# Modulation sums of a two-layer decoder trunk: scaling on ScalarE and accumulating DMAs instead of running sums on VectorE

## The chip, the cores and the metric

One core of one Trainium2 chip runs the whole kernel. The metric is the device time of one execution in microseconds (us); a time given for a kernel is the median of several runs. Five engines work beside each other, each with its own queue in order: TensorE (PE; the loads of its stationary operand are listed as PEld), VectorE (DVE), ScalarE (ACT), GpSimd (POOL) and SyncE (SP). SyncE issues nearly all DMAs of this kernel. Sixteen DMA engines carry them.

## The reference

The reference is a trunk of two layers on one sequence of 512 tokens with 2048 features, in float32. Layer 0 is differential attention with 8 heads and a SiLU gate; layer 1 is forgetting attention with 16 heads, on keys and values that are projected once from the stream. What the change touches is the modulation: a conditioning vector `c` gives, by matrix-vector products, a shift, a scale and a gate for each layer, and a shift and a scale for the shared keys and values.

```
c_act = silu(c)                                   # 1 x 2048
for l in range(2):
    mod = c_act @ w_mod[l] + b_mod[l]             # 2048 x 6144 for each layer
    shift, scale, gate = split(mod, 3)
    h = x * (1 + scale) + shift
    if l == 0:
        y = diff_attention(h, ...)
    else:
        mod = c_act @ w_mod_kv + b_mod_kv         # 2048 x 4096
        shift_kv, scale_kv = split(mod, 2)
        k, v, F = projections(x * (1 + scale_kv) + shift_kv)
        y = forgetting_attention(h, ..., k, v, F)
    x = layer_norm(alpha * x + gate * y)
```

## The kernel before

The contraction over 2048 features is cut into 16 k-tiles of 128. Large products are done in three matmuls each: an operand is split into a high part that TensorE takes as it is (`hi`, a cast on ScalarE) and the rest (`lo`, a subtraction on VectorE), and `products` adds high x high, low x high and high x low (lines 201 to 203).

Weights of the projections come through `WeightStream`: SyncE loads two k-tiles into a stage `wst` (four stages, line 59), ScalarE casts them into `whi` (line 106, three buffers), VectorE makes `wlo` (line 107, three buffers). `group` runs one projection block: eight such steps with four bursts of six matmuls each. After each burst, `tick` takes one prepared piece of attention work and a number `bg` of steps from the generator `background`. This is how the modulation is slipped in beside the matmuls.

The first 190 us make scale and shift of layer 0 with their own code. The rest of the modulation is made by two runs of the generator `mod_stream` (line 383), each over 12 column blocks of 512 columns:

- The first stream makes the gate of layer 0 and the shift and scale for keys and values, during layer 0's projections and attention (about 190 to 810 us). It loads two k-tiles at a time into `ms` (two buffers of 128 x 2 x 512).
- The second makes shift, scale and gate of layer 1, from the output projection of layer 0 on and through the projections of values (`vj`) and keys (`kj`), about 860 to 1325 us. It loads one k-tile at a time into `ms` (three buffers), and for loads 50 to 105 of the stream into buffers `msk` of a large pool, up to seven k-tiles ahead.

A block has one accumulator `macc` (128 x 512, two buffers). For each k-tile VectorE does one instruction: `macc = ms * cact[k] + macc` (line 420; the first k-tile of a block is a plain product, line 418), where `cact[k]` is a column of 128 scalars. A step of the generator is one k-tile. When 16 are done, `mod_rows` (line 440) transposes `macc` in 32 x 32 blocks into `mturn`, reduces along the rows into `mred`, and after four blocks one small matmul (line 460), an addition of the bias and a store to DRAM end one vector of 2048. The function `fold` later reads it back, in the second stream for the input of layer 1, and the gate is read back at the residual.

Outside the first stage the order of the instructions on each engine is chosen by a scheduler from the program's order and its dependencies; the sums are held in the program's order by `keep_in_program_order`. An engine executes its queue strictly in that order, so an instruction that waits holds up all that stand behind it. SyncE holds up the weight loads in the same way.

Of the kernel before, what the change touches and what calls it, by code (L numbers as in the profile page):

```python
# [137 lines left out]
def tile_yoco(  # L138
# [23 lines left out]
    nc = tc.nc  # L162
    V, S, PE, G = nc.vector, nc.scalar, nc.tensor, nc.gpsimd
# [19 lines left out]
    def acc_bank(name="acc"):  # L183
        return ps.tile([P, 512], F32, name=name, tag="acc", bufs=4)
# [4 lines left out]
    def tr_bank(name="tr"):  # L189
        return ps.tile([P, 512], F32, name=name, tag="tr", bufs=1)  # L190
# [39 lines left out]
    cact = const.tile([P, KT], F32, name="cact")  # L230
# [15 lines left out]
    rows = {}  # L246
# [44 lines left out]
    kk = Job(a_w_in, [(2048 + 128, 128), (2048 + 384, 128)])  # L291
# [88 lines left out]
        return const.tile([P, KT], F32, name=name)  # L380


    def mod_stream(segs, new_stage, new_acc, nk, deep=range(0), new_deep=None):

        todo = [(i, r) for i in range(len(segs)) for r in range(KT // nk)]
        loaded = {}
        summed = []

        def load(k):
            i, r = todo[k]
            src, col, _ = segs[i]
            t = new_deep() if k in deep else new_stage()
            rows = src[nk * r * P : nk * (r + 1) * P, col : col + 512]
            nc.sync.dma_start(t, rows.rearrange("(k p) n -> p k n", p=P) if nk > 1 else rows)
            loaded[k] = t

        def load_upto(k):
            n = len(loads)  # L400
            while n < len(todo) and n <= (k + 7 if n in deep else k + 2 // nk):
                load(n)
                loads.append(n)
                n += 1

        loads = []
        load_upto(-1)
        for k, (i, r) in enumerate(todo):
            load_upto(k)
            if r == 0:  # L410
                acc = new_acc()
            t = loaded.pop(k)
            for kk in range(nk):
                kt = nk * r + kk
                w = t[:, kk, :] if nk > 1 else t

                if kt == 0:
                    ins = V.tensor_scalar(acc, w, cact[:, 0:1], None, op0=ALU.mult)
                else:
                    ins = V.scalar_tensor_tensor(acc, w, cact[:, kt : kt + 1], acc, op0=ALU.mult, op1=ALU.add)  # L420
                tc.keep_in_program_order(ins)
                if kt == KT - 1:
                    summed.append(segs[i][2](acc))
                if kt in (1, 9) and summed:
                    if next(summed[0], None) is None:
                        summed.pop()
                yield
        for n, _ in enumerate(summed[0]):

            for _ in range(1 if n else 6):  # L430
                yield

    def four_ones(pool):

        t = pool.tile([P, P], F32, name="fours", tag="fours")
        for k in range(0, P, 32):
            S.copy(t[k : k + 32, 0:32], ident[k : k + 32, k : k + 32])
        return t[:, 0:32]

    def mod_rows(pool, fours, dst, bias, one):  # L440

        red = []

        def steps(n, acc):
            if n == 0:
                red.append(pool.tile([P, 64], F32, name="mred", tag="mred", bufs=2))
            t = pool.tile([P, 512], F32, name="mturn", tag="mturn", bufs=1)
            V.transpose(t, acc)  # L450
            V.tensor_reduce(
                red[0][:, 16 * n : 16 * n + 16], t.rearrange("p (j q) -> p j q", q=32), axis=mybir.AxisListType.X, op=ALU.add
            )
            if n == 3:
                row = pool.tile([64, 32], F32, name="mrow", tag="mrow", bufs=1)
                nc.sync.dma_start(row, bias.rearrange("(j q) -> j q", q=32))
            yield True
            if n == 3:
# [12 lines left out]
    with tc.tile_pool(name="start", bufs=2, reuse_waits="tile") as sp, tc.manual_schedule(engines=MANUAL):  # L471
# [10 lines left out]
        loads = []  # L482
# [319 lines left out]
    ap = actx.enter_context(tc.tile_pool(name="ap", bufs=1, reuse_waits="tile"))  # L802
    segs = []
    fours = four_ones(ap)
    for dst, src, col, bias, one in (
# [4 lines left out]
        steps = mod_rows(ap, fours, dst, bias[col : col + D], one)  # L810
        segs += [(src, col + 512 * f, partial(steps, f)) for f in range(4)]
    background = mod_stream(
        segs,
        lambda: ap.tile([P, 2, 512], F32, name="ms", tag="ms", bufs=2),
        lambda: ap.tile([P, 512], F32, name="macc", tag="macc", bufs=2),
        2,
    )
    dist = ap.tile([P, 512], F32, name="dist")
    G.iota(dist, pattern=[[-1, 512]], base=384, channel_multiplier=1, allow_small_or_imprecise_dtypes=True)
# [327 lines left out]
    def ktile(name):  # L1147
        return kpool.tile([P, T], F32, name=name, tag="K")
# [61 lines left out]
    def open_n():  # L1210
        nonlocal background
        actx.close()
        pool = nctx.enter_context(tc.tile_pool(name="npool", bufs=1, reuse_waits="tile"))
        zp.extend((pool, pool.tile([P, TB, D], F32, name="n"), pool.tile([P, TB, 4, 6], F32, name="nstats")))
        fours = four_ones(pool)
        segs = []
        for dst, col, one in ((mod_dram[1][0:1, :], 0, 0.0), (mod_dram[1][1:2, :], D, 1.0), (gate_dram[1], 2 * D, 0.0)):
            steps = mod_rows(pool, fours, dst, b_mod[1, col : col + D], one)
            segs += [(w_mod[1], col + 512 * f, partial(steps, f)) for f in range(4)]
        background = mod_stream(  # L1220
            segs,
            lambda: pool.tile([P, 512], F32, name="ms", tag="ms", bufs=3),
            lambda: pool.tile([P, 512], F32, name="macc", tag="macc", bufs=2),
            1,

            deep=range(50, 106),
            new_deep=lambda: ktile("msk"),
        )

    def end_of_sums():  # L1230
# [163 lines left out]
    acc = [acc_bank() for _ in range(TB)]  # L1394
# [4 lines left out]
    for i, (half, s) in enumerate(lag):  # L1399
# [299 lines left out]
```

## Time and profile before

| | us |
|---|---|
| median of three runs | 1944.55 |
| lowest and highest run | 1944.41, 1945.12 |
| span of the profiled execution | 1943.2 |
| TensorE busy | 1922.5 |
| VectorE busy | 1351.3 |
| ScalarE busy | 730.3 |
| GpSimd busy | 2.2 |

The span reaches from the first to the last instruction of one profiled execution. Consecutive matmuls overlap in the records (a matmul of 512 columns is recorded with some 0.39 us but they start every 0.23 us), so TensorE's busy time says that it always had one in hand, not how fast it worked. In a row of the groups, `out<-in` names the tile written and the tiles read, then come shapes, count, total busy time, the mean time of one in ns, and the time for which the engine stood idle just before, with whom it waited for. A row of DMA issues ends with the median time from issue to landing.

### The profile page before, as it was taken

Reading aid. Unit: us, or ns where it says so; the run is one execution under the profiler, and the core shown is the slowest. Engines: PE = TensorE matmul, PEld = TensorE weight load, DVE = VectorE, ACT = ScalarE, POOL = GpSimd, SP = SyncE. Lnnn points to the kernel's source line nnn. Section 1 sums busy time; section 2 is a strip of 40 time slices with the busy share of each in tenths; the row PEclk is TensorE's granted clock in tenths of the full one; section 3 lists DMA queues with packets and bytes.
Section 4 is the critical chain, followed back from the end, with each engine's and each line's share of the span. In section 5 each row is a group of like instructions: output and inputs, shape, how many; then the busy total and the mean of one; then the engine's idle time right before and its main releaser. Section 6 shows DMA issues by size and latency. Waiting matters only on the chain.

```text
span 1943.2 us, 25791 instructions
## 1 busy us (share of the span) xinstructions
PE 1922.5 (99%) x8973; PEld 1619.5 (83%) x8973; DVE 1351.3 (70%) x2514; ACT 730.3 (38%) x1250; POOL 2.2 (0%) x10
## 2 busy tenths in 40 slices
PE   8999999999999999999999999999999999999997
PEld 7888888888888888888889998888888888888886
DVE  6884588777676768567675657777566666677657
ACT  3546344323332334521273222224343434353123
POOL 0000000000000000000000000000000000000000
PEclk9999999999999999999999999999999999999999
DMA  9983466676767675377557756774355555554622
GB/s 339 383 300 115 151 187 201 210 230 188 239 192 225 202 237 167 121 241 225 171 174 256 266 187 214 251 260 158 118 154 148 153 155 154 152 171 153 222 91 105
DMA packets 351630, 382.19 MB, mean 197 GB/s; under 512 B 77926, under 2 KB 260860, under 8 KB 350732
## 3 DMA queue, kind: packets, MB, share of 16 engines
q1 hardware_dynamic: 348620, 376.35, 61.6%
q10 hardware_dynamic: 2880, 4.20, 0.6%
q8 instruction: 70, 1.15, 0.2%
q14 instruction: 60, 0.49, 0.1%
HBM read 348.65 MB, written 31.80 MB: 196 GB/s over the span
## 4 chain that ended last, share of the span: by engine, by line
PE 96%; DVE 3%; DMA 1%; issue 0%; ACT 0%; SPq 0%; DVEq 0%
PE acc L201 27%; PE acc L202 27%; PE acc L203 27%; PE acc L703 4%; PE sc L703 2%; PE o L201 1%; PE o L202 1%; PE o L203 1%; PE sc L203 1%; PE sc L202 1%; PE o L703 1%; PE sc L201 1%; DVE sacc L601 1%; PE tr L643 0%; PE tr L669 0%; PE tr L629 0%
## 5 line engine op out<-in xcount | busy, mean ns | idle before, releaser
L106 ACT CAST whi<-wst 128x1024 fp32r<-128x1024 f32 (+2 forms) x298 | 303.4, 1018 | 660.7 <-PE acc L203 353.2
L107 DVE TENSOR_TENSOR wlo<-wst,whi 128x1024 fp32r<-128x1024 f32 (+2 forms) x298 | 351.4, 1180 | 261.0 <-ACT whi L106 254.5
L201 PE MATMUL acc<-hh,whi 128*128 128x512 f32 x1184 | 463.5, 391 | 0.0
L202 PE MATMUL acc<-hl,whi 128*128 128x512 f32 x1184 | 461.8, 390 | 0.0
L203 PE MATMUL acc<-hh,wlo 128*128 128x512 f32 x1184 | 460.9, 390 | 0.0
L201 PE MATMUL acc<-whi,hh 128*128 128x512 f32 (+1 forms) x1168 | 444.4, 381 | 0.0
L202 PE MATMUL acc<-wlo,hh 128*128 128x512 f32 (+1 forms) x1168 | 442.3, 379 | 0.0
L203 PE MATMUL acc<-whi,hl 128*128 128x512 f32 (+1 forms) x1168 | 441.8, 378 | 0.0
L420 DVE SCALAR_TENSOR_TENSOR macc<-ms,cact,macc 128x512 f32<-128x512 f32 x307 | 229.1, 746 | 63.1 <-DMA ms<-in_w_mod_dram 41.1
L203 PEld LDWEIGHTS acc<-hh,wlo 128*128 128x128 f32 x1184 | 222.3, 188 | 47.6
L201 PEld LDWEIGHTS acc<-hh,whi 128*128 128x128 f32 x1184 | 222.5, 188 | 43.6 <-issue 0.6
L202 PEld LDWEIGHTS acc<-hl,whi 128*128 128x128 f32 x1184 | 222.4, 188 | 42.1
L203 PEld LDWEIGHTS acc<-whi,hl 128*128 128x128 f32 x1168 | 219.2, 188 | 36.5 <-DVE hl L1280 0.2
L201 PEld LDWEIGHTS acc<-whi,hh 128*128 128x128 f32 x1168 | 219.2, 188 | 34.8 <-DVE ztmp L1194 0.4
L202 PEld LDWEIGHTS acc<-wlo,hh 128*128 128x128 f32 x1168 | 219.3, 188 | 33.6 <-DVE wlo L107 0.3
L601 DVE SCALAR_TENSOR_TENSOR sacc<-sms,cact,sacc 128x512 f32<-128x512 f32 (+1 forms) x123 | 87.5, 712 | 5.9 <-DMA sms<-in_w_mod_dram 2.6
L880 ACT ACTIVATE e<-e,mn 128x128 f32<-128x128 f32 (+3 forms) x64 | 36.0, 563 | 113.5 <-DVE mn L876 99.6
L1504 ACT ACTIVATE eb<-eb,mnb 128x128 f32<-128x128 f32 (+1 forms) x64 | 36.0, 563 | 88.0 <-DVE mnb L1501 87.8
L876 DVE CUSTOM_DVE_ANT_0 e<-sc,bias 128x128 f32<-128x128 f32 (+3 forms) x64 | 31.0, 485 | 28.1 <-PE sc L203 27.8
L125 DVE TENSOR_TENSOR wlo<-wst,whi 128x768 fp32r<-128x768 f32 (+1 forms) x32 | 34.8, 1088 | 18.7 <-ACT whi L118 9.9
L703 PE MATMUL acc<-whi,hh 128*128 128x512 f32 x128 | 46.4, 394 | 0.0
L703 PE MATMUL acc<-whi,hl 128*128 128x512 f32 x128 | 45.9, 394 | 0.0
(285 smaller groups left out, 1999.0 us busy)
## 6 DMA issues: line engine op xcount, KB each, us to landing
wst<-in_a_w_in_dram SPq DMA_DIRECT2D x240, 256.0 KB, 4.1
ms<-in_w_mod_dram SPq DMA_DIRECT2D x136, 256.0 KB, 3.7
ms<-in_kv_w_mod_dram SPq DMA_DIRECT2D x64, 512.0 KB, 4.0
wst<-in_b_w_in_dram SPq DMA_DIRECT2D x128, 256.0 KB, 3.0
sms<-in_w_mod_dram SPq DMA_DIRECT2D x56, 512.0 KB, 7.7
wst<-in_kv_w_dram SPq DMA_DIRECT2D x40, 512.0 KB, 4.2
ms<-in_w_mod_dram SPq DMA_DIRECT2D x32, 512.0 KB, 4.5
wst<-in_a_w_out_dram SPq DMA_DIRECT2D x32, 512.0 KB, 4.4
```

The lines of the kernel that those rows point to most:

```text
L106: self.nc.scalar.copy(hi[:, :, :w], st[:, :, :w])
L107: self.nc.vector.tensor_tensor(lo[:, :, :w], st[:, :, :w], hi[:, :, :w].bitcast(F32), op=ALU.subtract)
L125: self.nc.vector.tensor_tensor(lo[:, :, :w], st[:, :, :w], hi[:, :, :w].bitcast(F32), op=ALU.subtract)
L201: PE.matmul(dst, lhs[0], rhs[0], start=start, stop=False)
L202: PE.matmul(dst, lhs[0], rhs[1], start=False, stop=False)
L203: PE.matmul(dst, lhs[1], rhs[0], start=False, stop=stop)
L420: ins = V.scalar_tensor_tensor(acc, w, cact[:, kt : kt + 1], acc, op0=ALU.mult, op1=ALU.add)
L601: V.scalar_tensor_tensor(acc, w, sc, acc, op0=ALU.mult, op1=ALU.add)
L703: PE.matmul(bank[n, bk], l, r, start=start, stop=stop, skip_group_check=True)
L876: V.tensor_tensor_reduce(out=e[:, :w], in0=sc[:, :w], in1=st["bias"][:, (3 - i) * P :], scale=-1.0, scalar=3.0e38, op0=ALU.add, op1=ALU.mi ...
L880: S.activation(e[:, :w], e[:, :w], AF.Exp, bias=mn, scale=-1.0, accum_out=rs)
L1504: S.activation(e[:, :w], e[:, :w], AF.Exp, bias=mn, scale=-1.0, accum_out=rs)
```

## The change

`mod_stream` now always loads two k-tiles at a time. The first pair of a block is loaded straight into the accumulator `macc`, which is now 128 x 2 x 512; the other seven pairs go into `ms`, 128 x 2 x 512 with two buffers, in both streams. ScalarE scales each half in place by its column of `cact`. When a pair other than the first is scaled, GpSimd issues one DMA from `ms` to `macc` that adds into its destination. The load of pair k+1 is issued when pair k is taken up; the separate, deeper buffers `msk` are gone. After a block, VectorE adds the two halves of `macc`, and one turn later transposes and reduces as before, in the accumulator's second half instead of `mturn`.

```diff
-    def mod_stream(segs, new_stage, new_acc, nk, deep=range(0), new_deep=None):
+    def mod_stream(segs, new_stage, new_acc):
-        todo = [(i, r) for i in range(len(segs)) for r in range(KT // nk)]
+        todo = [(i, r) for i in range(len(segs)) for r in range(KT // 2)]
...
         def load_upto(k):
-            n = len(loads)
-            while n < len(todo) and n <= (k + 7 if n in deep else k + 2 // nk):
-                load(n)
-                loads.append(n)
-                n += 1
+            for n in range(len(loads), min(k + 1, len(todo))):
+                i, r = todo[n]
+                src, col, _ = segs[i]
+                t = loaded[n] = new_stage() if r else new_acc()
+                rows = src[2 * r * P : 2 * (r + 1) * P, col : col + 512]
+                nc.sync.dma_start(t, rows.rearrange("(k p) n -> p k n", p=P))
+                loads.append(n)
...
+        load_upto(1)
         for k, (i, r) in enumerate(todo):
-            load_upto(k)
+            load_upto(k + 1)
+            t = loaded.pop(k)
             if r == 0:
-                acc = new_acc()
-            t = loaded.pop(k)
-            for kk in range(nk):
-                kt = nk * r + kk
-                w = t[:, kk, :] if nk > 1 else t
-                if kt == 0:
-                    ins = V.tensor_scalar(acc, w, cact[:, 0:1], None, op0=ALU.mult)
-                else:
-                    ins = V.scalar_tensor_tensor(acc, w, cact[:, kt : kt + 1], acc, op0=ALU.mult, op1=ALU.add)
-                tc.keep_in_program_order(ins)
-                if kt == KT - 1:
-                    summed.append(segs[i][2](acc))
-                if kt in (1, 9) and summed:
+                acc = t
+            for kk in range(2):
+                kt = 2 * r + kk
+                tc.keep_in_program_order(S.activation(t[:, kk, :], t[:, kk, :], AF.Copy, scale=cact[:, kt : kt + 1]))
+                if kk and r:
+                    G.dma_start(acc, t, accum_op=ALU.add)
+                if kt in (3, 5, 11) and summed:
                     if next(summed[0], None) is None:
                         summed.pop()
                 yield
+            if r == KT // 2 - 1:
+                summed.append(segs[i][2](acc))
...
-            t = pool.tile([P, 512], F32, name="mturn", tag="mturn", bufs=1)
-            V.transpose(t, acc)
+            t = acc[:, 1, :]
+            V.tensor_tensor(acc[:, 0, :], acc[:, 0, :], acc[:, 1, :], op=ALU.add)
+            yield True
+            V.transpose(t, acc[:, 0, :])
...
-            lambda: pool.tile([P, 512], F32, name="ms", tag="ms", bufs=3),
-            lambda: pool.tile([P, 512], F32, name="macc", tag="macc", bufs=2),
-            1,
-            deep=range(50, 106),
-            new_deep=lambda: ktile("msk"),
+            lambda: pool.tile([P, 2, 512], F32, name="ms", tag="ms", bufs=2),
+            lambda: pool.tile([P, 2, 512], F32, name="macc", tag="macc", bufs=2),
```

How the change stands in the queues is best seen where the second stream meets the projection of the keys. First ScalarE's queue there. Before, in the first key blocks, it holds the weight casts (line 106) and the copies of finished banks (line 1340). The names in brackets are the counters waited for: DMAHW those of SyncE's DMAs, DMASW those of GpSimd's, the others the engines'.

```order
L1340 COPY kT<-acc 128x512 [waits PE_49]
L106 COPY whi<-wst 128x1024 [waits DMAHW3_49,DVE_49,PE_49]
L106 COPY whi<-wst 128x1024 [waits DMAHW0_49,DVE_49,PE_49]
L106 COPY whi<-wst 128x1024 [waits DMAHW4_49,DVE_49,PE_49]
L106 COPY whi<-wst 128x1024 [waits DMAHW1_49,DVE_49,PE_49]
L106 COPY whi<-wst 128x1024 [waits DMAHW5_49,DVE_49,PE_49]
```

The same place after the change:

```order
L407 ACTIVATE ms<-ms,cact 128x512 [waits DMAHW3_49,DMASW3_49,Activation_49]
L407 ACTIVATE ms<-ms,cact 128x512
L106 COPY whi<-wst 128x1024 [waits DMAHW5_49,DVE_49,PE_49]
L407 ACTIVATE ms<-ms,cact 128x512 [waits DMAHW5_49,DMASW4_49,Activation_49]
L407 ACTIVATE ms<-ms,cact 128x512
L106 COPY whi<-wst 128x1024 [waits DMAHW7_49,DVE_49,PE_49]
L407 ACTIVATE ms<-ms,cact 128x512 [waits DMAHW0_49,DMASW5_49,Activation_49]
L407 ACTIVATE ms<-ms,cact 128x512
L106 COPY whi<-wst 128x1024 [waits DMAHW2_49,DVE_49,PE_49]
```

The two scalings of a pair (line 407) have moved in ahead of each weight cast, and the first of them waits for the load of its pair.

Next SyncE's queue in the same stage. Before, each weight load (line 59) stands among three or four loads of one k-tile (line 396), which wait for VectorE to have read the stage:

```order
L59 DMA wst<-in_kv_w_dram 128x2x512 [waits DVE_49]
L396 DMA ms<-in_w_mod_dram 128x512 [waits DMAHW4_49,DVE_49]
L396 DMA ms<-in_w_mod_dram 128x512 [waits DMAHW5_49,DVE_49]
L396 DMA ms<-in_w_mod_dram 128x512 [waits DMAHW6_49,DMAHW2_49,DVE_49]
L59 DMA wst<-in_kv_w_dram 128x2x512 [waits DVE_49]
```

After the change:

```order
L59 DMA wst<-in_kv_w_dram 128x2x512 [waits DVE_49]
L396 DMA ms<-in_w_mod_dram 128x2x512 [waits DMAHW4_49,DMASW6_49,Activation_49]
L59 DMA wst<-in_kv_w_dram 128x2x512 [waits DMAHW3_49,DVE_49]
L396 DMA ms<-in_w_mod_dram 128x2x512 [waits DMAHW0_49,DMASW7_49,Activation_49]
L59 DMA wst<-in_kv_w_dram 128x2x512 [waits DMAHW5_49,DVE_49]
L396 DMA ms<-in_w_mod_dram 128x2x512 [waits DMAHW6_49,DMAHW2_49,DMASW0_49]
L59 DMA wst<-in_kv_w_dram 128x2x512 [waits DMAHW7_49,DVE_49]
```

Between two weight loads there now stand one or two loads of a pair, and each waits for an accumulation (DMASW) that GpSimd issued.

GpSimd's queue was empty after its setup; in this stage it now holds:

```order
L409 DMA macc<-ms 128x1024 [waits DMASW0_49,DMAHW5_49,DVE_49,Activation_49]
L409 DMA macc<-ms 128x1024 [waits DMAHW7_49,DMASW0_49,Activation_49]
L409 DMA macc<-ms 128x1024 [waits DMAHW2_49,DMASW1_49,Activation_49]
L409 DMA macc<-ms 128x1024 [waits DMAHW4_49,DMASW2_49,Activation_49]
L409 DMA macc<-ms 128x1024 [waits DMAHW6_49,DMASW3_49,Activation_49]
```

Each waits for the one before it (DMASW counted up by one from row to row) and for ScalarE.

More of the change, by code (lines that the diff above doesn't have):

```diff
@@ L380, in cols @@
         return const.tile([P, KT], F32, name=name)
-    def mod_stream(segs, new_stage, new_acc, nk, deep=range(0), new_deep=None):
-        todo = [(i, r) for i in range(len(segs)) for r in range(KT // nk)]
[L388 to L397, printed above, removed]
-        def load_upto(k):
-            n = len(loads)
-            while n < len(todo) and n <= (k + 7 if n in deep else k + 2 // nk):
-                load(n)
+    def mod_stream(segs, new_stage, new_acc):
+        todo = [(i, r) for i in range(len(segs)) for r in range(KT // 2)]
+        loaded, loads, summed = {}, [], []
+        def load_upto(k):
+            for n in range(len(loads), min(k + 1, len(todo))):
[4 more added lines that the diff above has]
+                nc.sync.dma_start(t, rows.rearrange("(k p) n -> p k n", p=P))
@@ L403, in load_upto @@
                 loads.append(n)
-                n += 1
-        loads = []
-        load_upto(-1)
+        load_upto(1)
         for k, (i, r) in enumerate(todo):
-            load_upto(k)
+            load_upto(k + 1)
+            t = loaded.pop(k)
             if r == 0:
-                acc = new_acc()
-            t = loaded.pop(k)
-            for kk in range(nk):
-                kt = nk * r + kk
-                w = t[:, kk, :] if nk > 1 else t
-                if kt == 0:
-                    ins = V.tensor_scalar(acc, w, cact[:, 0:1], None, op0=ALU.mult)
-                else:
-                    ins = V.scalar_tensor_tensor(acc, w, cact[:, kt : kt + 1], acc, op0=ALU.mult, op1=ALU.add)
-                tc.keep_in_program_order(ins)
-                if kt == KT - 1:
-                    summed.append(segs[i][2](acc))
-                if kt in (1, 9) and summed:
+                acc = t
[5 more added lines that the diff above has]
+                if kt in (3, 5, 11) and summed:
@@ L814, in tile_yoco @@
         lambda: ap.tile([P, 2, 512], F32, name="ms", tag="ms", bufs=2),
-        lambda: ap.tile([P, 512], F32, name="macc", tag="macc", bufs=2),
-        2,
+        lambda: ap.tile([P, 2, 512], F32, name="macc", tag="macc", bufs=2),
     )
```

## The prediction

> **What bounds the kernel now.** I read the page's engine line first, then a table by stage, then TensorE's own waits in the stage where the two streams of sums run.
>
> ```profile
> span 1943.2 us, 25791 instructions
> PE 1922.5 (99%) x8973; PEld 1619.5 (83%) x8973; DVE 1351.3 (70%) x2514; ACT 730.3 (38%) x1250; POOL 2.2 (0%) x10
> ...
> 0.00:190.00 190.00, 182.47 (x847) 152.75 (x848) 136.85 (x199) 96.50 (x155) 2.17 (x10) 1.00 0.86 290
> 190.00:1330.00 1140.00, 1139.49 (x5379) 967.46 (x5378) 812.94 (x1549) 407.00 (x708) 0.00 (x0) 1.00 0.66 208
> 1330.00:1943.00 613.00, 600.57 (x2751) 499.31 (x2749) 401.53 (x767) 226.84 (x390) 0.00 (x0) 0.99 0.48 148
> ...
> PE sc L1286 <- ACT n L1261: 0.5, 1, 0.5
> ```
>
> The windows give start:end, length, busy time and count of PE, PEld, DVE, ACT and POOL, the granted clock, the DMA engines' busy share, GB/s. The sums lie in 190 to 1330 us. There TensorE is busy 1139.49 of 1140 us, and the last row is its only wait. So whatever VectorE is freed of, this stage can give back 0.5 us. The question is only whether the new route for the sums feeds ScalarE and SyncE as fast as TensorE consumes.
>
> **What is removed and added.** VectorE loses these groups:
>
> ```profile
> L420 DVE SCALAR_TENSOR_TENSOR macc<-ms,cact,macc 128x512 f32<-128x512 f32 x307 | 229.1, 746 | 63.1 <-DMA ms<-in_w_mod_dram 41.1 <-DMA ms<-in_kv_w_mod_dram 19.0
> L420 DVE SCALAR_TENSOR_TENSOR macc<-msk,cact,macc 128x512 f32<-128x512 f32 x53 | 39.7, 749 | 1.0
> L418 DVE TENSOR_SCALAR macc<-ms,cact 128x512 f32<-128x512 f32 x21 | 10.1, 479 | 1.2 <-DMA ms<-in_kv_w_mod_dram 1.2
> L1642 DVE TENSOR_TENSOR z<-nr,ztmp 128x512 f32<-128x512 f32 x16 | 10.5, 686 | 0.1
> L1062 ACT ACTIVATE ogs<-ogT,subg 128x512 f32<-128x512 f32 x14 | 9.1, 714 | 0.0
> ```
>
> 229.1 + 39.7 + 10.1 = 279 us (three more first products make 384 in all) go; 24 adds of one half to the other come, at 0.686 us (the L1642 row) 16 us. Both are worth nothing at the end: TensorE's matmuls cover them. Were they not covered, the 263 us would be the gain, but the 0.5 us row forbids that. ScalarE gains 384 scalings by a column; the nearest row is L1062, 0.714 us, so 274 us, and 407 + 274 = 681 of 1140 us is 60%. Its throughput is not the problem either.
>
> GpSimd's queue gains 168 accumulating DMAs of 512 KB (7 for each of 24 column blocks), and no row shows one. The loads become 192 of 512 KB instead of 288, but each of the 168 that fill a stage now waits for an accumulation. Call A the time from issuing an accumulation to its landing. Two waits repeat:
>
> *The chain*: accumulation r+1 reads and writes the tile that r writes, so it waits for r. One per A.
>
> *The ring*: there are two stage tiles. Load n needs the tile that accumulation n-2 reads; ScalarE needs load n; accumulation n needs ScalarE. Two accumulations per A + load + two scalings.
>
> ```profile
> ms<-in_kv_w_mod_dram SPq DMA_DIRECT2D x64, 512.0 KB, 4.0
> sms<-in_w_mod_dram SPq DMA_DIRECT2D x56, 512.0 KB, 7.7
> ms<-in_w_mod_dram SPq DMA_DIRECT2D x32, 512.0 KB, 4.5
> n_dram<-n SPq DMA_DIRECT2D x4, 1024.0 KB, 3.8
> out_dram<-z SPq DMA_DIRECT2D x7, 512.0 KB, 2.7
> ```
>
> (Last number: median us to landing.) A load is 4.2 (between 4.0 and 4.5), two scalings 1.4. The ring takes (A + 5.6)/2 for one accumulation, the chain A; the larger counts, T. They cross at A = 5.6.
>
> *The price of A*. From the two stores, another 512 KB costs 3.8 - 2.7 = 1.1 us, so 1.6 is fixed. An accumulation reads source and destination: 1.6 + 2 x 1.1 = 3.8 alone. It runs beside loads, and these take 4.0 to 4.5 where the store took 2.7: 1.3 to 1.8 us more for each 512 KB moved, 2.6 to 3.6 for two. That gives 6.4 to 7.4. I take **A = 6.6**, near the lower end because it starts in SBUF, as the cheaper stores do. Bounds: 2.7 (it costs no more than a store) and 1.6 + 2 x (7.7 - 1.6) = 13.8 (both halves move as slowly as the loads under full DMA). At 6.6 the chain decides, T = 6.6.
>
> The Trainium skill, "DMA: Bandwidth & Descriptors", section "Anatomy of one DMA — SWDGE (gpsimd) path", fits a transfer from GpSimd's queue at 2.0 us plus bytes over 436 GB/s. That is 3.2 us here for a plain copy; by it the ring would decide with T = 4.4 and the end would be 1961 us, an estimate from that page. No run so far shows it.
>
> **The pace it must keep.** One column block is 16 k-tiles and 7 accumulations, so a k-tile costs 7T/16 = 2.89 us at T = 6.6. The table shows how many k-tiles the kernel asks for now (DVE busy, its count, clock, DMA share, GB/s):
>
> ```profile
> 250.00:350.00 100.00, 21.63 (x30) 1.00 0.66 196
> 350.00:500.00 150.00, 45.23 (x62) 1.00 0.71 216
> 500.00:750.00 250.00, 70.98 (x98) 1.00 0.70 213
> 750.00:860.00 110.00, 9.39 (x13) 1.00 0.55 170
> 860.00:950.00 90.00, 28.35 (x39) 1.00 0.65 209
> 950.00:1025.00 75.00, 0.00 (x0) 1.00 0.51 165
> 1025.00:1050.00 25.00, 7.93 (x11) 1.00 0.77 257
> 1050.00:1150.00 100.00, 35.79 (x49) 1.00 0.77 259
> 1150.00:1200.00 50.00, 15.38 (x21) 1.00 0.58 178
> 1200.00:1325.00 125.00, 57.28 (x79) 1.00 0.75 249
> ...
> L106 ACT CAST whi<-wst 128x1024 fp32r<-128x1024 f32 x23 | 24.3, 1055 | 70.9 <-PE acc L202 66.3 <-DVE wlo L107 4.4
> ```
>
> k-tiles x 2.89 less the length: 62 make 179 us, 29 too many; 98: 283, 33; 39: 113, 23; 11: 32, 7; 49: 142, 42; 21: 61, 11; 79: 228, 103. The stretches with 30 and 13 k-tiles keep up. Sum 247 us. ScalarE and SyncE work in the order shown ahead of this text: behind a late scaling stand the whi casts that TensorE needs, behind a late load the weight loads. So lateness reaches TensorE one for one once ScalarE's lead is used up. That lead is two casts (three whi buffers; the last row, of 1200 to 1325 us, shows the casts waiting for TensorE to free one), at 125/23 = 5.4 us each 11 us, and it is filled again in the two slack stretches: three times 11 = 33 us off. 247 - 33 = **214 us**. The profiled execution spans 1943.2 and the median of the runs is 1.35 above it: 1943.2 + 214 + 1.35 = **2158 us**.
>
> By the bounds of A, in the same way: A = 2.7 gives T = 4.15, 1.82 us a k-tile; only the last stretch is late, by 18 - 11, so 1952. A = 13.8 is 6.04 us a k-tile: late by 1459 in all, so about 3370. Between them: A = 4.5 (T = 5.05) gives 1991; A = 8.9 is 624 - 33 = 591 us late, 2535.
>
> **The rivals.**
>
> *The accumulation is quick* (A under 4.5): 1952 to 1990. For it: the plain-copy fit of the Trainium skill's page named above, and the 2.7 us row. Against it: the stores of that row stand near the end, where the DMA engines are half idle. The ring still binds in the densest stretch.
>
> *It is slow* (A above 8.9): over 2535. For it: no row shows an adding DMA, nor one from GpSimd's queue. Against it: only the loads under full DMA, in the first stage, come near.
>
> *The 16 DMA engines are full* before chain or ring bind (A small, but all transfers late). Two moves of 1.1 us for each accumulation, on top of the shares in the table: 1200 to 1325 needs 0.75 x 125 + 34.6 x 2.2 = 170 us of all engines, 45 too many; 1050 to 1150 124, 24; the others 46 together (16, 19, 6, 5). 115 - 33 = 82: 2026 us. Deeper buffers would then not help. The Trainium skill, in the same page under "Issuing engines are not separate DMA queues", says that DMAs from all queues share the 16 engines, which speaks for it.
>
> *Not slower*: TensorE sees nothing. The place is the densest stretch: 79 k-tiles in 125 us ask for 1.58 us a k-tile, so T = 3.6 and, by the ring, A under 1.6 us, which is the fixed part of a store alone; the mechanism would be that loads and accumulations overlap more than the two tiles seem to allow. Then the time is 1944, at best 0.5 us less.
>
> **How the numbers follow.** The forecast (chain or ring, A from 4.5 to 8.9, 1990 to 2535, likeliest 2158) has 0.67; quick accumulation 0.06; slow 0.11; full DMA engines 0.10; not slower 0.06. The range 1985 to 2535 holds the forecast, the full engines and a little of the quick case, 0.8. A measurement here tells 0.2%, 4 us, from no change. Faster takes half of the not-slower case, 0.03, same the other half, 0.03; all else is slower, 0.94.
>
> **What would show it.** Right: POOL's DMAs from macc<-ms land in 4.5 to 8.9 us; SP's longest waits are loads of ms on them; ScalarE's idle time before ms<-ms,cact is on DMA and in the order of 200 us; TensorE loses its time between 350 and 750 us and, most of all, in the stretch that was 1200 to 1325, and nothing after the second stream. DMA share in those stretches stays under 1.0. Wrong: a DMA share at 1.0 with ring waits short (full engines); TensorE's waits naming VectorE (the adds or the transposes late); or a loss in the stage after 1330 us, where I expect none. If the landing of an accumulation is right but the time is not, the step from k-tiles to lateness is at fault.

## The result and the profile after

The change makes the kernel slower: 2366.94 us (median of 4 runs, 2363.09 to 2371.42) against 1944.48 us for the kernel before on the same chip (4 runs, 1943.96 to 1945.12). The ratio is 1.2173, with a 95% interval of 1.2159 to 1.2187. So 422 us were lost. The prediction was a loss of 214 us, 2158 us in all, in a range of 1985 to 2535: the range holds the time, and the loss came out nearly twice as large as forecast.

First the page of the kernel after: the span, the engines' busy time, the granted clock and the DMA engines' share in 40 slices, and the chain that ended last, by engine and by line.

```profile
span 2366.0 us, 25982 instructions
...
PE 2030.7 (86%) x8973; PEld 1682.8 (71%) x8973; DVE 1114.0 (47%) x2154; ACT 958.3 (41%) x1634; POOL 145.1 (6%) x178
...
PEclk9999998898988989998898888787779999999999
DMA  9964888888988978487758888787864445455632
...
PE 31%; DMA 29%; DVE 3%; issue 2%; ACT 2%; SPq 0%; POOLq 0%; DVEq 0%; ACTq 0%
DMA macc<-ms 24%; PE acc L201 9%; PE acc L202 9%; PE acc L203 9%; DMA ms<-in_w_mod_dram 3%; DMA e<-turned 1%; ACT ms L407 1%; ACT whi L106 1%; PE o L201 1%; DVE wlo L107 1%; PE o L202 1%; PE o L203 1%; PE sc L203 0%; PE sc L202 0%; PE sc L2
```

TensorE's busy time plus its idle time is the span. Before, 20.7 of 1943.2 us were idle; now 2366.0 - 2030.7 = 335.3 are. That is 314.6 us of the loss. The other 108 us (2030.7 - 1922.5) are busy time of the same 8973 matmuls, whose records became longer (391 ns on average before and 411 after in the largest group of line 201); they go with the slices where the clock row falls below 9. VectorE became freer by 237 us (1351.3 to 1114.0), and nothing came of it. The chain points to the cause: the DMAs from `ms` to `macc` alone hold 24% of the span, where the kernel before had no such thing. (The shares of the chain add up to some two thirds: it was not followed back to the start.)

The groups show what the added work does to its own engines: the scalings on ScalarE, GpSimd's DMA instructions, and VectorE's addition of the two halves (busy time, mean ns, idle time before them and its releaser).

```profile
L407 ACT ACTIVATE ms<-ms,cact 128x512 f32<-128x512 f32 x336 | 230.0, 716 | 628.0 <-DMA ms<-in_w_mod_dram 481.9
...
L409 POOL DMA_DIRECT2D macc<-ms x168 | 142.9, 851 | 1453.1 <-DMA macc<-ms 571.2
L438 DVE TENSOR_TENSOR macc<-macc 128x512 f32<-128x512 f32 x24 | 16.6, 692 | 163.3 <-DMA macc<-ms 163.3
```

The scaling costs 0.716 us, as the prediction took it from another row (0.714), and the addition of halves 0.692 (0.686). GpSimd's instruction, which no row had shown, takes 0.851 us of the engine, one for each DMA. The DMA issues and the queue give the price that everything hung on (packets, MB and share of the 16 engines for the queue; KB and median us to landing for the issues):

```profile
q0 software_dynamic: 24192, 88.09, 19.4%
...
macc<-ms POOLq DMA_DIRECT2D x168, 512.0 KB, 7.2
...
ms<-in_w_mod_dram SPq DMA_DIRECT2D x112, 512.0 KB, 4.1
...
ms<-in_kv_w_mod_dram SPq DMA_DIRECT2D x56, 512.0 KB, 3.9
```

An accumulation lands 7.2 us after its issue (4.4 at least, 9.8 at most). It keeps the 16 DMA engines busy for 19.4% x 2366.0 / 168 = 2.73 us. The waits show how this spreads (us in total, times, longest): GpSimd waits for its own last accumulation, ScalarE for the loads, VectorE's `wlo` for the casts that stand behind the scalings (254.5 us in the kernel before), and TensorE for the casts.

```profile
DVE wlo L107 <- ACT whi L106: 649.9, 171, 15.1
POOL macc L409 <- DMA macc<-ms: 571.2, 80, 9.4
ACT ms L407 <- DMA ms<-in_w_mod_dram: 481.9, 98, 9.6
...
PE acc L201 <- ACT whi L106: 41.4, 14, 7.9
```

The casts are only one of TensorE's waits. It waits 54.9 us for attention values of ScalarE (`ah`), 35.5 and 22.4 us for ScalarE's copies of finished `kT` and `vt` banks, and 44.1 us for a gate (`sg`) of VectorE. So the lateness reaches it through much of ScalarE's work, and not through the weight casts alone.

SyncE's queue, in its own view, holds the `ms` loads back until an accumulation has read the tile:

```profile
SPq L396 <- DMA macc<-ms: 744.8, 140, 9.3
```

Now a piece of the chain in the second stream, in the projection of the keys (start, length, what):

```profile
1500.15 6.91 DMA macc<-ms
1507.06 0.03 POOLq L409
1507.09 0.49 issue
1507.58 9.05 DMA macc<-ms
1516.62 0.03 POOLq L409
1516.65 0.49 issue
1517.14 8.06 DMA macc<-ms
...
1525.21 4.11 DMA ms<-in_w_mod_dram
```

The accumulations follow one another. The next one starts 0.52 us after the last has landed (0.03 + 0.49 us), and between the three accumulations no engine's work appears. That is the *chain* of the prediction, with a hand-over that the prediction had not counted. Three stretches, with the columns as in the prediction and GpSimd's busy time and count ahead of the clock:

```profile
500.00:600.00 100.00, 84.53 (x381) 69.29 (x381) 41.57 (x93) 45.19 (x79) 11.37 (x14) 0.93 0.92 236
1460.00:1765.00 305.00, 207.72 (x770) 160.37 (x769) 82.14 (x115) 106.89 (x155) 33.28 (x39) 0.81 0.79 198
1800.00:2366.00 566.00, 553.63 (x2543) 460.67 (x2541) 380.94 (x737) 210.23 (x368) 0.00 (x0) 0.99 0.48 150
```

From 1460 to 1765 us, the densest stretch of the second stream, GpSimd issued 39 accumulations, one in 305 / 39 = 7.82 us: 7.2 for landing on average and about 0.5 for the hand-over. By the start and the landing of each, 28 of the 39 start 0.52 us after the one before has landed; most of the others stand at the start of a block, where a new accumulator begins. Over the whole streams it is 58 of 83 steps in the second and 49 of 83 in the first, where more of them wait for a scaling. TensorE is busy for 208 of the 305 us. The DMA engines are at 0.79 there, and at 0.92 between 500 and 600 us, in the first stream. After the last accumulation TensorE has its 554 of 566 us again.

Where the loss arises is read from three landmarks of the order, which stands alike in both kernels. Before (the end of each row gives the first and the last start):

```profile
L1194 DVE TENSOR_TENSOR ztmp<-acc,gate x32: 652/682/693, 844.5 to 1931.1; 128x512 f32<-128x512 f32 x32
...
L1240 DVE SCALAR_TENSOR_TENSOR n<-xr,ztmp x16: 676/684/694, 846.1 to 983.6; 128x512 f32<-128x512 f32 x16
...
L1340 ACT COPY kT<-acc x16: 575/589/591, 1205.8 to 1342.1; 128x512 f32<-128x512 f32 x16
```

After:

```profile
L1183 DVE TENSOR_TENSOR ztmp<-acc,gate x32: 649/681/692, 1006.0 to 2353.8; 128x512 f32<-128x512 f32 x32
...
L1225 DVE SCALAR_TENSOR_TENSOR n<-xr,ztmp x16: 676/682/694, 1007.5 to 1198.1; 128x512 f32<-128x512 f32 x16
...
L1325 ACT COPY kT<-acc x16: 563/576/591, 1523.1 to 1763.4; 128x512 f32<-128x512 f32 x16
```

The first `ztmp` follows the first stream: it starts 161.5 us later. The last write of `n` ends the stage where the second stream begins: 214.5 us later. The last `kT` ends the keys' projection: 421.3 us later. So 161, 53 and 207 us, and nothing behind.

### The profile page after: what moved, and what is told of

It is laid out like the page before. It is cut to its first block, busy times and chain, and to the rows that moved or that the text cites. A ratio compares the mean times of both kernels' runs of the same rounds, so it can differ in the third digit from the quotient of the medians.

```text
span 2366.0 us, 25982 instructions
## 1 busy us (share of the span) xinstructions
PE 2030.7 (86%) x8973; PEld 1682.8 (71%) x8973; DVE 1114.0 (47%) x2154; ACT 958.3 (41%) x1634; POOL 145.1 (6%) x178
## 3 DMA queue, kind: packets, MB, share of 16 engines
q0 software_dynamic: 24192, 88.09, 19.4%
## 4 chain that ended last, share of the span: by engine, by line
PE 31%; DMA 29%; DVE 3%; issue 2%; ACT 2%; SPq 0%; POOLq 0%; DVEq 0%; ACTq 0%
DMA macc<-ms 24%; PE acc L201 9%; PE acc L202 9%; PE acc L203 9%; DMA ms<-in_w_mod_dram 3%; DMA e<-turned 1%; ACT ms L407 1%; ACT whi L106 1%; PE o L201 1%; DVE wlo L107 1%; PE o L202 1%; PE o L203 1%; PE sc L203 0%; PE sc L202 0%; PE sc L201 0%
## 5 line engine op out<-in xcount | busy, mean ns | idle before, releaser
L107 DVE TENSOR_TENSOR wlo<-wst,whi 128x1024 fp32r<-128x1024 f32 (+2 forms) x298 | 351.1, 1179 | 660.2 <-ACT whi L106 649.9
L201 PE MATMUL acc<-hh,whi 128*128 128x512 f32 x1184 | 486.9, 411 | 103.6 <-DVE sg L837 44.1
L201 PE MATMUL acc<-whi,hh 128*128 128x512 f32 (+1 forms) x1168 | 459.8, 394 | 78.7 <-DVE ztmp L1183 36.9
L203 PE MATMUL acc<-hh,wlo 128*128 128x512 f32 x1184 | 480.9, 406 | 11.3 <-DVE wlo L107 10.9
L407 ACT ACTIVATE ms<-ms,cact 128x512 f32<-128x512 f32 x336 | 230.0, 716 | 628.0 <-DMA ms<-in_w_mod_dram 481.9
L202 PE MATMUL acc<-hl,whi 128*128 128x512 f32 x1184 | 480.1, 406 | 0.0
L202 PE MATMUL acc<-wlo,hh 128*128 128x512 f32 (+1 forms) x1168 | 456.6, 391 | 24.3 <-DVE wlo L107 24.3
L409 POOL DMA_DIRECT2D macc<-ms x168 | 142.9, 851 | 1453.1 <-DMA macc<-ms 571.2
L438 DVE TENSOR_TENSOR macc<-macc 128x512 f32<-128x512 f32 x24 | 16.6, 692 | 163.3 <-DMA macc<-ms 163.3
L201 PE MATMUL o<-vh,ah 128*128 128x256 f32 x80 | 25.6, 320 | 55.0 <-ACT ah L919 54.9
L201 PEld LDWEIGHTS o<-vh,ah 128*128 128x128 f32 x80 | 16.5, 207 | 60.1 <-ACT ah L919 59.3
```

Source lines behind the costliest of these rows:

```text
L107: self.nc.vector.tensor_tensor(lo[:, :, :w], st[:, :, :w], hi[:, :, :w].bitcast(F32), op=ALU.subtract)
L201: PE.matmul(dst, lhs[0], rhs[0], start=start, stop=False)
L202: PE.matmul(dst, lhs[0], rhs[1], start=False, stop=False)
L203: PE.matmul(dst, lhs[1], rhs[0], start=False, stop=stop)
L407: tc.keep_in_program_order(S.activation(t[:, kk, :], t[:, kk, :], AF.Copy, scale=cact[:, kt : kt + 1]))
L409: G.dma_start(acc, t, accum_op=ALU.add)
```

## The experiments

Theory: one accumulation at a time on one accumulator sets the pace, some 7.7 us each (the chain). Rivals: the two stage tiles set it (the ring); the 16 DMA engines are full; ScalarE's added scalings cost the time. A second question was what makes an accumulation so long: adding, size, GpSimd's queue, or the company of other DMAs.

| kernel | us | ratio to before | 95% interval |
|---|---|---|---|
| the change | 2366.94 | 1.2173 | 1.2159 to 1.2187 |
| e1, copied and not added | 2172.94 | 1.1169 | 1.1150 to 1.1187 |
| e2, added by VectorE | 1947.97 | 1.0017 | 1.0007 to 1.0026 |
| e3, DMAs of half the size | 2257.12 | 1.1607 | 1.1587 to 1.1627 |
| e4, four stage tiles | 2377.76 | 1.2226 | 1.2208 to 1.2244 |
| e5, two accumulators in turns | 2252.67 | 1.1582 | 1.1557 to 1.1607 |
| e6, first stream only | 2117.24 | 1.0881 | 1.0864 to 1.0899 |
| e7, second stream only | 2201.75 | 1.1322 | 1.1303 to 1.1341 |
| e8, copied, issued by ScalarE | 2144.56 | 1.1027 | 1.1009 to 1.1046 |
| e9, trims alone | 2377.15 | 1.2219 | 1.2199 to 1.2239 |

### e2: the scalings without the DMAs

```diff
-                    G.dma_start(acc, t, accum_op=ALU.add)
+                    tc.keep_in_program_order(V.tensor_tensor(acc, acc, t, op=ALU.add))
```

> ScalarE scales as in the change, but VectorE adds each scaled pair (128x1024) to the accumulator and GpSimd's queue stays empty. Theory (only the accumulating DMAs cost): 1944 to 1955 us. Rival (the scalings ahead of the weight casts in ScalarE's queue cost by themselves): above 1980 us.

1947.97 us (10 runs, 1946.86 to 1948.85), 3.3 us above before. TensorE's row and the new group of VectorE:

```profile
PE 1924.5 (99%) x8973; PEld 1620.5 (83%) x8973; DVE 1304.9 (67%) x2322; ACT 965.2 (50%) x1634; POOL 2.2 (0%) x10
...
L409 DVE TENSOR_TENSOR macc<-macc,ms 128x1024 f32<-128x1024 f32 x168 | 205.2, 1221 | 98.9 <-ACT ms L407 98.2
```

All 384 scalings stand on ScalarE as in the change, the loads have the same size and the same two tiles, and TensorE still has its 1924.5 us with hardly a pause. So the scalings, the larger loads and the shorter stage, with additions on VectorE, cost 3 us in all. The other 419 us come with the accumulating DMAs in place of these additions.

### e6 and e7: one stream at a time

In e6 the first stream has the change and the second is that of the kernel before; in e7 it is the other way round.

```diff
...
-    background = mod_stream(
+    background = mod_stream_dma(
...
```

> Only the first stream is made by ScalarE and accumulating DMAs; the second is as before. Theory (lateness arises stage by stage and is never caught up): the loss is what the trace of the change shows at the first output projection, 161 us, so 2090 to 2125 us. Rival (part of the lag is caught up, or the second stream alone makes the loss): under 2050 us.

> Only the second stream is made by ScalarE and accumulating DMAs; the first is as before. Theory: 423 - 161 = 262 us lost, 2190 to 2225 us, and with the run of the first stream alone the two losses add up to the whole one within 20 us. Rival (the streams share something): the two losses miss the sum by more.

Both came as expected: +172.5 us for the first stream, +257 us for the second. The sum, 429.6, is within 8 us of the whole loss: the two streams lose on their own, and neither pays for the other. How much each loses is shown by this; what sets the pace inside a stream is tested below for the second alone.

### e4, e5 and e9: a deeper ring, or two chains

Both kernels change the second stream alone. To make room, some temporaries get one buffer where they had two. e4 has four stage tiles and loads three pairs ahead; e5 keeps two tiles and lets the pairs go to two accumulators in turns, which VectorE adds at the end (156 accumulations in all, since two pairs of a block are loaded straight into them). So e5 changes two things: the order on one accumulator, and the number of accumulations, which is 72 instead of 84 in the second stream.

```diff
 (e4)
-            lambda: pool.tile([P, 2, 512], F32, name="ms", tag="ms", bufs=2),
+            lambda: pool.tile([P, 2, 512], F32, name="ms", tag="ms", bufs=4),
...
 (e5)
-                if kk and r:
-                    G.dma_start(acc, t, accum_op=ALU.add)
+                if kk and r >= chains:
+                    G.dma_start(accs[r % chains], t, accum_op=ALU.add)
...
+            for other in accs[1:]:
+                V.tensor_tensor(acc, acc, other, op=ALU.add)
```

> In the second stream four stage buffers instead of two and loads up to three pairs ahead; to make room for it three small temporaries of that stage have one buffer instead of two. Theory (the chain through the accumulator sets the pace): 2340 to 2375 us, no more than 1% off the change. Rival (the ring through the stage buffers does): the second stream's part of the loss shrinks and the time falls below 2300 us. Rival (the 16 DMA engines are full): no change either, but then their share in 1300 to 1750 us is 0.95 or more.

> In the second stream two accumulators for a block, taken in turns by the pairs, so that an accumulation waits for the one before the last; six accumulations for a block instead of seven, two stage buffers as in the change, and the same three temporaries with one buffer. Theory (chain): the ring of two stages takes over at (7.7 + 5.6)/2 = 6.7 us instead of 7.7, and with six for seven the time falls by about 130 us, to 2210 to 2260 us. Rival (DMA engines full): only the seventh accumulation is saved, 2320 us or more.

The ring of four took 2377.76 us, 11 us above the change: within the 1% that the theory gave, and 3 us above the range written for it. Only a control could tell whether the deeper stage or the trims did this:

> Control for the two kernels with other buffers in the second stream: the change as it is (two stage tiles, one accumulator), with only the trimmed temporaries of those kernels (tn, htmp2, htmp and layer 0's ztmp with one buffer each). If the trims cost nothing, the time is the change's, 2362 to 2372 us, and the ring of four's extra 11 us come from its deeper stage. If the trims cost something themselves, the time is near 2378 us, and the gain of two chains is larger by as much than it looked.

The trims alone took 2377.15 us. So they cost 10 us, and twice the stage tiles are worth nothing that can be told from none (0.6 us between the two, well inside both intervals). e5 came out inside its expectation; against the same control it gains 2377.15 - 2252.67 = 124.5 us, where the second stream's whole loss is 257.

How much of this gain is the order? Twelve accumulations fewer, at the change's 7.82 us each, would by themselves be worth 94 us, an estimate, which leaves some 30 us. The pace says the same: in the dense part the control issues 51 accumulations in 400 us, one in 7.8 us, and e5 47 in 340 us, one in 7.2 us; 72 of them at 0.6 us less would be 43 us. So most of the gain comes from having fewer accumulations, and the order on one accumulator is shown to be worth only some 30 to 45 us with two stage tiles. The windows of the dense part, first of the control e9, then of e4, then of e5:

```profile
1300.00:1700.00 400.00, 283.54 (x1178) 240.72 (x1179) 76.64 (x87) 135.24 (x199) 43.27 (x51) 0.83 0.83 211
```

```profile
1300.00:1700.00 400.00, 263.35 (x1167) 228.64 (x1166) 77.25 (x88) 136.45 (x197) 43.44 (x51) 0.81 0.82 207
```

```profile
1300.00:1640.00 340.00, 279.12 (x1185) 235.18 (x1183) 102.85 (x127) 141.40 (x207) 39.91 (x47) 0.89 0.91 243
```

With four tiles the DMA engines stay at 0.82, TensorE is busy for 263 of 400 us, and there are 51 accumulations again: more data in stock was not what lacked. The chain is tighter there (68 of 83 steps of the second stream start 0.52 us after a landing, 58 in the control), but an accumulation of that stream lands after 8.2 us at the median, against 7.5 in the control; why it takes longer was not measured apart. With two chains the share is 0.91 and the `ms` loads take longer than in the change (4.8 in place of 4.1 us):

```profile
macc<-ms POOLq DMA_DIRECT2D x156, 512.0 KB, 6.7
...
ms<-in_w_mod_dram SPq DMA_DIRECT2D x100, 512.0 KB, 4.8
```

Two accumulations are now in flight together (they start 2.9 us apart at 1441.84 and 1444.77 us, the next two at 1455.31 and 1458.44), so the chain is cut. What GpSimd waits for between 1300 and 1640 us is no longer the last accumulation but the scalings (256.5 us, 43 times), that is the ring of two that e5 keeps. The rival of the full DMA engines comes near as well, at 0.91; how much either holds back was not measured apart. A ring of four together with two chains was not run, nor was a deeper ring in the first stream.

### e1 and e8: what adding and the queue cost

```diff
 (e1)
-                    G.dma_start(acc, t, accum_op=ALU.add)
+                    G.dma_start(acc, t)
...
 (e8)
-                    G.dma_start(acc, t, accum_op=ALU.add)
+                    nc.scalar.dma_start(acc, t)
```

> The DMAs from GpSimd's queue copy the scaled pair over the accumulator and do not add; the sums of all but the first and last pairs are left out. Everything else, the waits too, stays. Theory (an accumulation is dear because it reads two tiles): landing falls from 7.2 to about 5 us, the time to 2000 to 2060 us. Rival (it is GpSimd's queue and the trip that cost, not the adding): landing stays near 7 us and the time near 2367 us.

> As in e1_plain_copy the pair is copied over the accumulator and not added, so the sums are left out; here ScalarE issues the copy, behind its own scalings, where e1 had GpSimd issue it (5.3 us to landing, 2172.9 us). Theory: much of the price sits in the transfer from GpSimd's queue, whatever it does with the data. Then the copy lands in 2.7 to 3.8 us, like the stores that SyncE issues, and the ring takes (3.3 + 5.6)/2 = 4.5 us in place of 5.5: a sixth less for each accumulation, the time falls to 2020 to 2080 us. Rival: moving 512 KB within SBUF beside the loads is the price, whoever issues it. Then landing stays at 5.0 to 5.5 us and the time at 2140 to 2200 us.

e1 took 2172.94 us, in between what was expected of it by the one theory and the other; the landing came close to what the first theory said, the time did not. Its queue and its landing:

```profile
q0 software_dynamic: 24192, 88.09, 10.3%
...
macc<-ms POOLq DMA_DIRECT2D x168, 512.0 KB, 5.3
```

Without adding, the same 512 KB land in 5.3 us in place of 7.2, and take 10.3% x 2170.6 / 168 = 1.33 us of the 16 engines in place of 2.73. GpSimd's instruction falls from 0.85 to 0.53 us. So adding costs 1.9 us of the 7.2, and twice the engine time; most of the price is there without it. A piece of its chain, and two rows of GpSimd's own (start, length, and in brackets the idle time before and whom the profile names for it):

```profile
1436.80 0.71 ACT ms L407
...
1437.80 6.50 DMA macc<-ms
...
1444.83 6.81 DMA macc<-ms
...
1451.70 4.41 DMA ms<-in_w_mod_dram
...
1456.84 0.72 ACT ms L407
...
1457.87 5.99 DMA macc<-ms
```

```profile
1452.18 0.53 POOL L409 DMA_DIRECT2D macc<-ms  x1 [6.81 <-DMA macc<-ms]
...
1464.39 0.53 POOL L409 DMA_DIRECT2D macc<-ms  x1 [5.99 <-ACT ms L407]
```

Two waits show here. Where the scaling is last, the copy starts 0.29 us behind it (1437.51 to 1437.80). Where the landing of the last copy is last, the next starts 0.53 us behind that (1444.30 to 1444.83, 1451.64 to 1452.18, 1463.86 to 1464.39). In 1400 to 1560 us 20 of 26 copies start 0.53 us after a landing, though for 11 of these the profile names the scaling. In these 11 the scaling had ended only 0.31 to 0.37 us before, so it would have held the copy up by almost as much. The *chain* and the *ring* nearly tie, then, close to where the prediction lets them cross (A = 5.6), with the chain still ahead as its link has the hand-over too. There is one copy in 6.15 us, where the link is 5.3 + 0.53 = 5.8 us at the median and the ring by the prediction's formula (5.3 + 5.6)/2 = 5.5.

e8 took 2144.56 us, 28 us less than e1, with a landing that is no shorter (the trace has it for 59 of the 168 copies):

```profile
macc<-ms ACTq DMA_DIRECT2D x168, 512.0 KB, 5.9
```

The copy from ScalarE's queue takes 5.9 us, so GpSimd's queue is not what makes it long; that theory falls. The time is within what the rival gave, the landing a little above it. Where the chain differs from e1's is the hand-over, here from scaling to copy:

```profile
1185.55 1.34 ACT ms L407 x2
1186.89 0.04 issue
1186.93 5.87 DMA macc<-ms
```

Between the scalings and the copy lie 0.04 us, where e1 has 0.29; the engine that scales also issues. Behind a landing the next copy of e8 starts after about 0.1 us, where e1 has 0.53. The shorter hand-overs fit the gain; that they make up all 28 us was not measured apart.

### e3: half the size

VectorE adds the two halves of a pair, and GpSimd's DMA adds 256 KB. The addition of halves at the end of a block falls away.

```diff
+                if kk:
+                    tc.keep_in_program_order(V.tensor_tensor(t[:, 0, :], t[:, 0, :], t[:, 1, :], op=ALU.add))
                 if kk and r:
-                    G.dma_start(acc, t, accum_op=ALU.add)
+                    G.dma_start(acc[:, 0, :], t[:, 0, :], accum_op=ALU.add)
...
-            V.tensor_tensor(acc[:, 0, :], acc[:, 0, :], acc[:, 1, :], op=ALU.add)
```

> VectorE adds the two scaled halves of a pair, and the accumulating DMA carries 256 KB instead of 512 KB; as many of them, in the same chain. If landing is mostly moving of bytes, it falls from 7.2 to about 4.4 us, the ring of two stages then sets 5 to 5.6 us for each, and the time is 1990 to 2040 us. If it is mostly fixed, landing stays above 6 us and the time above 2200 us.

2257.12 us: neither expectation is met in full. The queue and the landing:

```profile
q0 software_dynamic: 24192, 44.05, 11.2%
...
macc<-ms POOLq DMA_DIRECT2D x168, 256.0 KB, 5.9
```

The engines' time follows the size: 11.2% x 2259.6 / 168 = 1.51 us in place of 2.73. The landing hardly does: 5.9 in place of 7.2 us. By these two points 2.6 us of the 7.2 go with the size and 4.6 do not, whatever is moved. The two runs differ in pace and in what runs beside, and in e3 VectorE's addition stands between the scaling and the DMA, so this is an estimate.

## Why the prediction held, and where its steps failed

**The bound and the gain.** Right. TensorE could give back 0.5 us and VectorE's relief was worth nothing: e2 has the scalings and no DMA, and no run came out below before.

**The mechanism.** Right for the second stream: the chain, not the ring. The next accumulation waits for the last and starts 0.52 us after its landing (28 of 39 in the dense stretch); four stage tiles change nothing (e4 against e9); and with two accumulators the waits for the last accumulation give way to waits for scalings (e5). In the first stream, which makes 172.5 us of the loss, no run has tested it: there 49 of 83 steps are links of the chain, and the DMA engines are at 0.92 between 500 and 600 us. The signs that were to show it are there: SyncE's longest waits are the `ms` loads on accumulations (744.8 us), landings are within 4.5 to 8.9 us at the median, the DMA share is under 1.0, and nothing is lost after the second stream.

**The size.** Here steps failed, and the loss was nearly twice the forecast one. The first is the term A, with the T that it gives. The prediction put 6.6 us; a landing took 7.2, and 0.5 us of hand-over that the prediction left out come on top: 7.82 us for each in the dense stretch, so 7 x 7.82 / 16 = 3.42 us a k-tile.

The second is the table of k-tiles. Its counts are of all VectorE instructions on `macc`, and these include one transpose for each block:

```profile
L450 DVE STREAM_TRANSPOSE mturn<-macc 128x512 f32<-128x512 f32 x24 | 16.9, 705 | 0.3
```

So 24 of the 402 in the table are no k-tiles. By lines 418 and 420 alone the stretches ask for 28, 59, 92, 12, 37, 0, 10, 46, 20 and 74. At T = 6.6 these give 186 us where the prediction has 247, and its time would have been 2098 us. The overcount moved the forecast toward the measured time, by luck.

With the right counts and 3.42 us a k-tile the late stretches are late by 52, 65, 37, 9, 57, 18 and 128: 366 us, or 333 less the 33 of ScalarE's lead, where 422 were measured. By stage, without the lead, that is 117, 37 and 212 us, and the landmarks show 161, 53 and 207. In the last stage the step from k-tiles to lateness thus holds to within 5 us, though T was read from the same run there. Over the first two stages the sum is 60 us short. From 354.8 to 932.5 us the first stream issues one accumulation in 8.1 us (71 steps) although its landing is shorter, 6.8 us at the median; more of them wait for scalings that are late themselves. What holds these up was not followed further and stays open. Nothing shows the lead of 33 us: taking it off makes the sum worse.

**How A was made up.** Here the parts failed worse than the sum. The prediction had 1.6 us fixed and, at A = 6.6, 5.0 that go with the bytes (two moves, and the sharing). By the estimate from e3 it is about 4.6 and 2.6: nearly the reverse. By e1 the second move and the addition cost 1.9 us together. Two errors of 3.0 and 2.4 us nearly cancelled, by luck. Whoever had used the split to choose a size, half a pair at a time, would have hoped for 4.1 us and found 5.9.

**The quick accumulation.** Wrong, and the prediction had given it a chance of 0.06. The page "DMA: Bandwidth & Descriptors" of the Trainium skill, section "Anatomy of one DMA — SWDGE (gpsimd) path", gives 2.0 us plus bytes over 436 GB/s, by which 512 KB would take 3.2 us, an estimate. The measured landings are longer: a plain copy from GpSimd's queue took 5.3 us at the median here, and an accumulation 7.2, beside loads in all cases.

**The full DMA engines.** Not the bound (0.79 in the dense stretch), though the price of one accumulation there was too low in the prediction: 2.73 us of all engines, where two moves of 1.1 gave 2.2. At the pace of the chain they are not asked for more; with two chains in the second stream they reach 0.91. For the first stream, at 0.92 in one stretch, the rival was not tested apart.

**Two signs that misled.** ScalarE's idle time before the scalings was to be some 200 us, and was 628. Idle time in front of a group is not lateness: ScalarE had slack ahead of the change (730.3 busy of 1943.2 us), and an engine with slack waits at whatever comes late. TensorE's waits do name VectorE as well, which the prediction had set down as a sign against it (the adds or the transposes late). But VectorE's `wlo` itself waits 649.9 us for casts of ScalarE (254.5 before), which stand behind late scalings; and where TensorE waits 21.4 us for a reduction, the addition of halves ahead of it waits for the last accumulation of its block (163.3 us in all). A wait has to be followed to its source before it counts.

**The ring.** In the change it does not decide in the second stream. In e1, with A at 5.3 us, chain and ring nearly tie, so the crossing at 5.6 was about right. The formulas leave out the hand-overs, 0.53 us behind a landing and 0.29 us behind a scaling, and they matter there.

## What to carry to other kernels

An accumulating DMA of this size was a link of 7 to 8 us, hand-over included, and in this kernel the links on one accumulator did not overlap: count them by (links x link time), against the time that the matmuls beside them leave, before the relief of VectorE is counted at all. More buffers ahead of this chain were worth nothing. By the estimate from e5 fewer links were worth most; a second accumulator let links overlap and gave less, with the ring of two tiles behind it. And check what a count of instructions contains before it enters a sum. And what is freed on an engine that the bounding engine never waits for is worth nothing, however many microseconds it is.

## What the runs showed of the hardware

By these runs more than half of a DMA between two tiles does not go with its size, an estimate from two sizes: 256 KB added in 5.9 us, 512 KB in 7.2, and 512 KB merely copied in 5.3 (from GpSimd) and 5.9 (from ScalarE), where SyncE's store of 512 KB to DRAM near the end of the kernel takes 2.7. Whether the destination in on-chip memory or the traffic beside it makes the difference was not measured apart.

Adding doubles the time that the 16 DMA engines spend on the same bytes (2.73 against 1.33 us); that the destination has to be read too fits this, and no run shows it apart. Its DMA instruction also holds GpSimd for 0.85 us, where a copy's holds it for 0.53.

The granted clock falls where TensorE has to wait: 0.81 in 1460 to 1765 us, 0.99 afterwards. The page "TensorE: Matmul & The Clock Gate" of the Trainium skill, in its part on the HAM clock gate, says that the clock is halved after an idle window of some 3.4 us. The trace agrees in the main: its clock records know only 1 and 0.5, and most of the falls stand right behind a pause of TensorE longer than that (the longest is 22.7 us), a few behind pauses of 2 to 3 us. The busy time of the matmuls is longer by 108 us with it. In the dense stretch this costs little, because the chain there is 90% DMA (81.4% `macc`, 9.0% `ms`).
